# Storing the first chunk of results of a pooling kernel as soon as it is rooted

## The chip, the core and the metric

The kernel runs on one core of a Trainium2 chip. The metric is the device time of one execution in microseconds (us). Several executions are made and the median is quoted. A single core shows no pair of dies to compare, so a run's state ("fast" or "slow") is told only by its time against the fastest run of the same kernel: over 1.5% above it counts as slow.

Engines named below: ACT (ScalarE), DVE (VectorE), SP (SyncE, which here only issues DMAs). "ACTq" and "SPq" in the profile are the sequencers of ACT and SP issuing a DMA.

## The reference

```python
batch, channels, length = 32, 256, 4096          # x: float32, 134.2 MB
kernel_size, p = 4, 2.0
window = np.abs(x[:, :, start:end]) ** p          # four neighbours
result[:, :, i] = (np.mean(window, axis=-1)) ** (1.0 / p)   # out: 33.6 MB
```

The output is the root of the mean square of each four neighbours.

## The kernel before

The flat input is cut into 22 loads (18 of 13,184 columns on each of 128 partitions, four smaller ones at the end). The loads form 11 groups, mostly two loads each; a group's input and its output are contiguous in HBM for each partition. Each load is worked off in chunks: ACT squares in place, DVE sums four neighbours into the output tile, ACT takes the root. There are three input slots and two output tiles.

```python
W, O_W = 13184, 6592
X_SLOTS, O_SLOTS = 3, 2
slots = [[(W, [4416, 4384, 4384])]] * 18          # one load a slot, three chunks a load
...
groups = [2] * 9 + [3, 1]
late = {7, 8, 9, 10}                              # stored at the very end, from SP
...
def store(g, queue):
    queue.dma_start(out=block(of, g, k), in_=ots[g])

def root(g, o, ends):
    nc.scalar.activation(out=o, in_=o, func=Act.Sqrt, scale=1.0 / k)
    if ends and g not in late:
        store(g, nc.scalar)                       # one store a group, from ACT
...
for step in chunks:
    nc.scalar.activation(out=v, in_=v, func=Act.Square)
    nc.vector.tensor_reduce(out=o, in_=v.rearrange("p (n j) -> p n j", j=k), ...)
    if pending is not None:
        root(*pending)                            # the root of the chunk before
    pending = (g, o, ...)
```

Loads are issued from SP (`nc.sync.dma_start`), the stores of groups 0 to 6 from ACT. The two use different DMA queues (on the page q1 with 144.15 MB, the loads and the late stores from SP, and q10 with 23.63 MB, the stores from ACT).

## Time and profile before

| what | value | where it is read |
|---|---|---|
| time, median of 3 (394.69 to 394.88) | 394.79 us | runs |
| span of the profiled run | 393.0 us | page |
| bytes moved, mean rate | 167.79 MB, 427 GB/s | page |
| DVE busy, ACT busy | 72%, 74% | page |
| packets of one engine: 52,736 B (load), 26,368 B (store) | 1.947 us, 0.978 us | packet records of the trace |
| first packet starts, last one ends | 1.74 us, 391.71 us | packet records |

The first fence is the part of the page of the kernel before that cuts the span into 40 equal slices. The digits are tenths of busy time; DMA is the mean over sixteen DMA engines; the last row is what they moved.

```profile
DVE  0068989494959495949594959595859686899992
ACT  1099986777786768686958695959595949899991
DMA  8999999999999999999999999999999999999997
GB/s 344 429 429 440 429 424 381 443 459 429 413 440 435 429 427 432 429 440 441 437 448 421 432 462 435 392 429 472 429 413 451 425 429 429 424 429 427 438 429 329
```

The DMA row is 9 in all slices but the first and the last. DVE and ACT alternate between 9 and 4 to 6: they wait for data (ACT waited 86.3 us in sum for loads). So the kernel is bound by data movement. The packet records agree: 52,736 B in 1.947 us are 27.1 GB/s for an engine and 433 GB/s for sixteen, and 167.79 MB at that rate take 387.2 us of the 393.0.

The next fence is from the chain that ended last, in order of time: start, duration, what. (A line "issue" of 0.02 us before the last one is left out.)

```profile
123.51 4.73 DVE ot L110
128.26 39.98 DMA xt<-in_x_dram
168.26 3.88 ACT xt L108
```

It looks as if a load waited for DVE. It did: DVE freed an input slot and the load was issued at 128.26. But it took 40 us to land, while one load's bytes need 15.6 us at the full rate. Its first packet started at 148.56 us, 20.3 us after the issue: until then the packets of the load before it ran (128.13 to 147.45 us), and from 137.85 us on those of a store beside them. So, as an estimate from these times, a load could have been issued many microseconds later without landing later; compute has slack.

The DMA issues of the page: operands, sequencer, count, size of each, median us from issue to landing (all bytes have arrived).

```profile
xt<-in_x_dram SPq DMA_DIRECT2D x18, 6592.0 KB, 39.7
out_dram<-ot ACTq DMA_DIRECT2D x7, 3296.0 KB, 26.4
```

Last, two stretches early in the run and two around the first store (its packets run from 59.6 to 81.9 us): from:to, length, DVE busy, ACT busy, POOL busy, clock, DMA share, GB/s.

```profile
29.00:36.00 7.00, 6.45 (x2) 6.25 (x4) 0.00 (x0) 1.00 1.06 460
36.00:49.00 13.00, 11.87 (x4) 12.93 (x6) 0.00 (x0) 1.00 0.94 402
57.00:65.00 8.00, 7.40 (x3) 7.97 (x4) 0.00 (x0) 1.00 1.03 392
65.00:82.00 17.00, 11.50 (x3) 11.74 (x6) 0.00 (x0) 1.00 1.04 451
```

The engines are busy throughout, but at the beginning of the first store they move less. There the packet records show load packets of up to 3.1 us instead of 1.947; this is called the slow patch below. (Packets are counted where they start, so a short stretch can read above the full rate.)

### The profile page before, as it was taken

Reading aid. Unit: us, or ns where it says so; the run is one execution under the profiler, and the core shown is the slowest. Engines: PE = TensorE matmul, PEld = TensorE weight load, DVE = VectorE, ACT = ScalarE, POOL = GpSimd, SP = SyncE. Lnnn points to the kernel's source line nnn. Section 1 sums busy time; section 2 is a strip of 40 time slices with the busy share of each in tenths; the row PEclk is TensorE's granted clock in tenths of the full one; section 3 lists DMA queues with packets and bytes.
Section 4 is the critical chain, followed back from the end, with each engine's and each line's share of the span. In section 5 each row is a group of like instructions: output and inputs, shape, how many; then the busy total and the mean of one; then the engine's idle time right before and its main releaser. Section 6 shows DMA issues by size and latency. Waiting matters only on the chain.

```text
span 393.0 us, 316 instructions
## 1 busy us (share of the span) xinstructions
DVE 282.4 (72%) x62; ACT 292.4 (74%) x126; POOL 0.2 (0%) x4
## 2 busy tenths in 40 slices
DVE  0068989494959495949594959595859686899992
ACT  1099986777786768686958695959595949899991
POOL 0000000000000000000000000000000000000000
DMA  8999999999999999999999999999999999999997
GB/s 344 429 429 440 429 424 381 443 459 429 413 440 435 429 427 432 429 440 441 437 448 421 432 462 435 392 429 472 429 413 451 425 429 429 424 429 427 438 429 329
DMA packets 4754, 167.79 MB, mean 427 GB/s; under 512 B 528, under 2 KB 528, under 8 KB 656
## 3 DMA queue, kind: packets, MB, share of 16 engines
q1 hardware_dynamic: 3744, 144.15, 85.3%
q10 hardware_dynamic: 1008, 23.63, 14.0%
q14 instruction: 2, 0.02, 0.0%
HBM read 134.22 MB, written 33.55 MB: 427 GB/s over the span
## 4 chain that ended last, share of the span: by engine, by line
DMA 62%; ACT 19%; DVE 14%; issue 2%; ACTq 0%; SPq 0%
DMA xt<-in_x_dram 62%; ACT xt L108 15%; DVE ot L110 11%; DVE xt L110 3%; ACT ot L84 3%; ACT xt L84 1%; ACTq L81 0%; SPq L75 0%; ACTq L108 0%
## 5 line engine op out<-in xcount | busy, mean ns | idle before, releaser
L110 DVE TENSOR_REDUCE ot<-xt 128x1096 f32<-128x4384 f32 (+1 forms) x54 | 255.4, 4731 | 102.7 <-ACT xt L108 102.4
L108 ACT ACTIVATE xt<-xt 128x4384 f32<-128x4384 f32 (+3 forms) x62 | 230.3, 3716 | 89.2 <-DMA xt<-in_x_dram 86.3
L84 ACT ACTIVATE ot<-ot 128x1096 f32<-128x1096 f32 (+1 forms) x54 | 59.8, 1108 | 1.8 <-DVE ot L110 0.9
L110 DVE TENSOR_REDUCE xt<-xt 128x824 f32<-128x3296 f32 (+1 forms) x8 | 27.0, 3384 | 1.3 <-ACT xt L108 1.2
L84 ACT ACTIVATE xt<-xt 128x824 f32<-128x824 f32 (+1 forms) x8 | 6.7, 841 | 3.0 <-DVE xt L110 2.9
L108 ACT ACT_TABLE_LOAD x1 | 1.3, 1283 | 0.7 <-PEq L137 0.7
L84 ACT ACT_TABLE_LOAD x1 | 1.3, 1283 | 0.0
L137 POOL MEMSET const-bfloat16-1.0<- 128x1 bf16 x1 | 0.1, 101 | 0.0
L137 POOL MEMSET const-uint8-127<- 128x1 uint8 x1 | 0.1, 101 | 0.0
L137 POOL MEMSET const-float32-0.0<- 128x1 f32 x1 | 0.1, 98 | 0.2 <-issue 0.2
L137 POOL MEMSET const-float32-1.0<- 128x1 f32 x1 | 0.1, 98 | 0.0
## 6 DMA issues: line engine op xcount, KB each, us to landing
xt<-in_x_dram SPq DMA_DIRECT2D x18, 6592.0 KB, 39.7
out_dram<-ot ACTq DMA_DIRECT2D x7, 3296.0 KB, 26.4
xt<-in_x_dram SPq DMA_DIRECT2D x3, 3296.0 KB, 24.6
out_dram<-ot SPq DMA_DIRECT2D x2, 3296.0 KB, 29.6
xt<-in_x_dram SPq DMA_DIRECT2D x1, 2528.0 KB, 26.4
out_dram<-xt SPq DMA_DIRECT2D x1, 2472.0 KB, 9.3
out_dram<-xt SPq DMA_DIRECT2D x1, 632.0 KB, 5.0
```

The source lines that it names most:

```text
L84: nc.scalar.activation(out=o, in_=o, func=Act.Sqrt, scale=1.0 / k)
L108: nc.scalar.activation(out=v, in_=v, func=Act.Square)
L110: nc.vector.tensor_reduce(out=o, in_=v.rearrange("p (n j) -> p n j", j=k), axis=mybir.AxisListType.X, op=mybir.AluOpType.add,)
L137: nc = _bacc.Bacc("TRN2", target_bir_lowering=False, num_devices=1)
```

## The change

The results of the first chunk of group 0 (1,104 columns, 4,416 B per partition) are stored as soon as they are rooted, at about 30 us instead of 56 us. The rest of group 0 (21,952 B per partition) follows in a second store at the group's end. The intent is that stores begin earlier. All other groups are stored as before.

```diff
-    def store(g, queue):
-        queue.dma_start(out=block(of, g, k), in_=ots[g])
+    stored = {}
+
+    def store(g, queue, until=None):
+        first = stored.get(g, 0)
+        until = columns[g] // k if until is None else until
+        queue.dma_start(out=block(of, g, k)[:, first:until], in_=ots[g][:, first:until])
+        stored[g] = until
 
     def root(g, o, ends):
         nc.scalar.activation(out=o, in_=o, func=Act.Sqrt, scale=1.0 / k)
         if ends and g not in late:
             store(g, nc.scalar)
+        elif g == 0 and g not in stored:
+            store(g, nc.scalar, o.shape[1])
```

## The prediction

> **What bounds the kernel.** Data movement. On the page the DMA row reads 9 nearly everywhere; DVE is busy 72%, ACT 74% of the 393.0 us. Packet by packet, a load packet of 52,736 B takes 1.947 us and a store packet of 26,368 B 0.978 us in almost every case: 433 GB/s for sixteen engines. [...] 167.79 MB at 433 GB/s are 387.2 us. From the first packet (1.74 us) to the last end (391.7 us) the engines are idle for a fraction of a microsecond in sum. The other 5.8 us: 1.7 us before the first packet, 1.3 us after the last, about 2.0 us of packets slower than normal, and small per-packet costs. Slow packets sit in three places: the first load (0.65 us per engine), reads drifting slower at 36 to 56 us (0.26 us), and reads at 57 to 61 us, where the first store starts (0.99 us). No later store has such a patch.
>
> The chain of waits shows 62% DMA. Its ACT and DVE pieces are not exposed compute: each releases a load 40 us before that load lands, and the transfer queued ahead of it takes the first 20 us.
>
> **What the change does.** Bytes stay the same. The first store (26,368 B per partition, issued at 55.6 us) becomes 4,416 B at about 29.7 us and 21,952 B where it was: one DMA more.
> - DMA: 8 packets more per engine. From 26,368 B (0.978 us), 19,776 B (0.735 us) and 5,056 B (0.194 us) I estimate a fixed part of 7 ns in a packet, so 0.06 us in all.
> - ACT: one more issue, 0.37 us, and a drain of 0.1 us, at 30 us. About 10 us of slack there, so 0 on the path.
> - The added DMA rotates which completion semaphores later DMAs reuse; in the order of the instructions no load gets a wait on something recent.
> - The early 0.57 MB (1.3 us of the full rate) enters the read stream. [...] its eight 0.16 us packets per engine spread over about 17 us. Load 1 lands a few tenths later, load 2 about 1.3 us later, the rest of the store is 1.3 us shorter, so loads from the fifth on are where they were.
>
> **Critical path.** It is the sum of the packets. A store cannot fill idle DMA time, since there is none, and the last bytes are untouched. What can move is slow-packet time: the 0.99 us at the first store should move to 30 to 35 us, about unchanged, and the 0.26 us of drift may go, since after the first store none is seen. Sum: +0.06 - 0.25, about -0.2 us.
>
> **Predicted: 394.6 us, 8 in 10 between 393.7 and 395.6.** Faster by over 2%: 1%; within 2%: 98%; slower by over 2%: 1%.
>
> **What would show it.** Mean rate about 427 GB/s; DMA share 9 throughout; 128 data packets more on the ACT queue; 4,416 B packets of about 0.17 us starting near 31 us; one slow patch at 31 to 36 us and none at 57 us; last packets end at about 391.5 us; issues from the sixth load on within 0.5 us of before.
>
> **What would make it wrong.** If each of the two stores pays its own slow patch, about +1 us. If the patch scales with the first store's packets, about -0.8 us. [...] If a semaphore reuse holds a load back for over 15 us, more.

Passages that did not come from the traces of this case are cut and marked. +0.06 - 0.25 comes to -0.19 us, and 394.6 us stands as forecast. The "about 17 us" is the estimate from packet times, 8 x (1.947 + 0.16) us, as if each store packet of an engine waited for one load packet. The trace of the kernel before shows about that: while the packets of its second store ran (98.94 to 119.25 us), 112 load packets and 128 store packets started.

## The result and the profile after

The changed kernel took 394.92 us (median of 6, 394.78 to 395.09), the kernel before 394.80 us (median of 6, 394.69 to 395.12). The ratio is 1.0002, 95% interval 0.9989 to 1.0015: the same. (Here and below a ratio is the mean time of one kernel's fast runs over that of the other's of the same rounds, so not quite the ratio of the medians quoted.)

The slices of the changed kernel:

```profile
DMA  8999998999999999999999999999999999999997
GB/s 343 429 429 447 453 434 366 472 397 434 421 464 424 461 434 400 464 434 430 394 464 426 432 432 432 426 429 442 429 425 434 461 451 429 400 429 428 436 424 304
```

The DMA row is what it was but for one 8 at the seventh slice: there was no idle time for an early store to fill.

The beginning of the early store, from the timeline of the changed kernel (start, duration, engine, line, operation; in brackets the idle time before):

```profile
28.51 1.12 ACT L90 ACTIVATE ot<-ot 128x1104 f32<-128x1104 f32 x1
29.67 0.37 ACTq L86 DMA_DIRECT2D out_dram<-ot  x1
30.09 3.86 ACT L116 ACTIVATE xt<-xt 128x4384 f32<-128x4384 f32 x1 [0.45 <-ACT ot L90]
```

ACT loses 0.45 us, with no consequence. And the issues of the loads, of the stores of the other groups and of the two stores of group 0, in the columns used before:

```profile
xt<-in_x_dram SPq DMA_DIRECT2D x18, 6592.0 KB, 39.7
out_dram<-ot ACTq DMA_DIRECT2D x6, 3296.0 KB, 27.1
out_dram<-ot ACTq DMA_DIRECT2D x1, 2744.0 KB, 27.4
out_dram<-ot ACTq DMA_DIRECT2D x1, 552.0 KB, 20.7
```

This is the line to remember. The small store has a sixth of the bytes, and still needs 20.7 us to land against 27. Its packets start at 33.72 us and end at 48.14 us, 14.4 us for 0.57 MB that the engines could move in 1.3 us. In the stretch from 34 to 48 us the packet records hold 111 load packets (5.85 MB) and 108 store packets (0.48 MB): the two queues take turns packet by packet, although a load packet here has 52,736 B and a store packet 4,416 B.

The stretches that answer to those of before:

```profile
29.00:36.00 7.00, 5.89 (x2) 5.99 (x4) 0.00 (x0) 1.00 0.90 382
36.00:49.00 13.00, 12.17 (x3) 12.93 (x6) 0.00 (x0) 1.00 1.10 470
57.00:65.00 8.00, 7.47 (x2) 7.58 (x4) 0.00 (x0) 1.00 0.92 370
65.00:82.00 17.00, 12.05 (x4) 12.31 (x7) 0.00 (x0) 1.00 1.01 438
```

The dip is at 57 to 65 us still, where the second, large piece starts, although a store has already run at 34 to 48 us. The prediction had put it at 31 to 36 us. The low 382 GB/s at 29 to 36 us is not it: load packets slower than usual make only 0.1 us per engine there, and the two early stretches together move more than before (an effect of counting packets where they start).

What each part came to, in us per engine, worked out from the packet records (excess: packet times over the usual 1.947 us for load packets):

```
                                      before    after
store packets of group 0, 8 or 16       7.82     7.89    (0.978 | 0.171 + 0.815 each)
excess, first 20 us                     0.69     0.75
excess, 28 to 54 us                     0.26     0.22
excess, 56 to 66 us                     0.99     0.54
excess, whole run                       2.02     1.62
last packet ends at                   391.71   391.96
```

The slow packets became fewer by 0.4 us, the added packets cost 0.07 us, and yet the last packet ended 0.25 us later in the profiled run. Such sums are not good to a few tenths, because an engine's packets overlap at their edges (up to 19 were in flight on 16 engines), and the sixteen engines finish unevenly (within 0.6 us before, 1.0 us after). Time without a packet, between the first and the last, is 0.9 us per engine before and 1.5 us after, which is about what the sums leave open. The timed runs say that all of it together is nothing, to within 0.15%.

### The profile page after: what moved, and what is told of

Its sections match the earlier page's. It is cut to its first block, busy times and chain, and to the rows that moved or that the text cites. A ratio compares the mean times of both kernels' runs of the same rounds, so it can differ in the third digit from the quotient of the medians.

```text
span 393.3 us, 318 instructions
## 1 busy us (share of the span) xinstructions
DVE 282.4 (72%) x62; ACT 292.7 (74%) x126; POOL 0.2 (0%) x4
## 3 DMA queue, kind: packets, MB, share of 16 engines
q1 hardware_dynamic: 3744, 144.15, 85.1%
## 4 chain that ended last, share of the span: by engine, by line
DMA 58%; ACT 21%; DVE 16%; issue 2%; another core or an unknown queue 1%; ACTq 0%; SPq 0%
DMA xt<-in_x_dram 58%; ACT xt L116 17%; DVE ot L118 12%; DVE xt L118 3%; ACT ot L90 3%; ACT xt L90 1%; ACTq L86 0%; SPq L76 0%; ACTq L116 0%
```

## The experiments

Theory A: the DMA engines are never idle, the time is the sum of the packets, and when a store is issued does not matter. Rival B: an early start gains something, and the extra store loses as much. Later, theory R: the turns of the two queues decide when many small stores do harm; rival S: each added store costs a fixed time, by its issue, its semaphore or its small packets.

### The kernel before, again

No edit; a control for the noise and for the slow patch.

> The kernel before, unchanged, as a control: the size of the noise, and whether the slow patch of read packets at the first store (0.99 us per engine, at 57 to 61 us) comes back. Theory A (the DMA engines are never idle, so the time is the sum of the packets and the moment of a store does not matter): ratio 1.000 within 0.0015; total packet time per engine 390.3 us within 0.5. If the patch is of the schedule it is at 57 to 61 us again, 0.7 to 1.3 us; if it is chance it moves or changes by half.

It took 394.83 us, ratio 0.9998 (0.9986 to 1.0010). The slow patch came back at 56 to 61 us with 1.04 us per engine. So it belongs to the schedule and is not chance. The other excess is not so steady: the 0.26 us at 28 to 54 us is 0.01 us in this run of the same kernel.

### Two pieces, both at the group's end

```diff
         if ends and g not in late:
+            if g == 0:
+                store(g, nc.scalar, 1104)
             store(g, nc.scalar)
-        elif g == 0 and g not in stored:
-            store(g, nc.scalar, o.shape[1])
```

> The added store without the early start: group 0 is stored in the same two pieces, both at the group's end. Theory A: 394.9 us, equal to the changed kernel within 0.5 us. Rival B (an early start gains about 1 us, as much as the pieces of the early data, and the extra store [...] loses it again, so that the two cancel): here only the loss is left, about 396 us. The slow patch: if it belongs to the first store of any size, it is at 57 to 61 us before packets of 4,416 B; if it belongs to large store packets, it comes later, before those of 21,952 B.

It took 394.89 us, ratio 0.9998 (0.9986 to 1.0010). Rival B falls: without the early start there is no loss that a gain would have had to cancel. The slow patch now has 0.15 us at 58 to 66 us, among the packets of 4,416 B (57 to 72 us), and 0.68 us at 72 to 77 us, around the first of 21,952 B (from 74.5 us). In this run most of it comes with the first large store packets.

### The early piece dropped

```diff
         elif g == 0 and g not in stored:
-            store(g, nc.scalar, o.shape[1])
+            stored[g] = o.shape[1]
```

> The first chunk's results are never stored (a wrong result on purpose), the rest of group 0 as in the changed kernel. Theory A: the time falls by the packet time of the piece, 8 x 0.171 us = 1.4 us, to 393.5 us (ratio to before about 0.9967). Rival C (a rate limit that is not the sum of the packets, or a path elsewhere, on which the piece has no weight): no change, 394.9 us.

It took 393.61 us, ratio 0.9967 (0.9955 to 0.9979), 1.2 us less where 1.4 were expected. Rival C of the expectation falls: bytes count, and the piece's packet time is nearly what it is worth. This also bounds what any move of that piece could gain: not moving it at all gains 0.3%.

### Every chunk stored as it is rooted

The change carried through groups 0 to 6: 42 stores in place of 7.

```diff
-        elif g == 0 and g not in stored:
-            store(g, nc.scalar, o.shape[1])
+        elif g not in late:
+            store(g, nc.scalar, stored.get(g, 0) + o.shape[1])
```

> Every chunk of groups 0 to 6 is stored as soon as it is rooted: 35 stores more than before, 280 packets more per engine. Theory A, with 7 ns of fixed time in a packet: +2.0 us, 396.8 us (ratio 1.005), DVE and ACT waits larger but off the path. Rival B (early stores gain): under 394 us. If ACT's extra issues (about 0.45 us each, 16 us in sum) were on the path: over 400 us, which theory A excludes.

It took 429.36 us, ratio 1.0882 (1.0845 to 1.0920). Theory A missed by far: the loss was 34.6 us and not 2. Rival B missed too. "Over 400 us" was met in the number, but the 16 us of added issues that it rested on are not half of the loss. The slices of this run:

```profile
ACT  1299897125998834199999244999999900399994
DMA  9999999999999999978999998989999999139956
GB/s 381 401 459 435 424 424 424 424 429 399 416 376 449 424 425 439 412 308 330 363 440 463 452 430 375 352 372 413 424 433 420 426 429 426 81 121 412 412 235 295
```

The first 17 slices are full, then idle time appears, above all from 367 us on (slices 35, 36 and 39). In the packet records an engine is without a packet for 31 us in sum, against 0.9 us before. So "the DMA engines are never idle" is not a property of the kernel that stores leave alone. Its timeline around 84 to 105 us:

```profile
84.25 0.34 ACTq L86 DMA_DIRECT2D out_dram<-ot  x1
84.63 3.86 ACT L116 ACTIVATE xt<-xt 128x4384 f32<-128x4384 f32 x1 [10.27 <-DMA out_dram<-ot]
88.39 1.11 ACT L90 ACTIVATE ot<-ot 128x1104 f32<-128x1104 f32 x1
101.41 0.34 ACTq L86 DMA_DIRECT2D out_dram<-ot  x1
101.79 3.86 ACT L116 ACTIVATE xt<-xt 128x4384 f32<-128x4384 f32 x1 [12.29 <-DMA out_dram<-ot]
```

ACT stands at a store's issue until an older store has landed, and starts nothing else for 10 to 12 us; in the whole run it waited so seven times, 66.1 us in sum. (The DMAs of the program share eight completion semaphores in the traces. The store issued at 84.25 us has the semaphore of one that landed at 84.17, the store issued at 101.41 that of one that landed at 101.33.) The issues show why the older stores are late:

```profile
out_dram<-ot ACTq DMA_DIRECT2D x28, 548.0 KB, 38.2
out_dram<-ot ACTq DMA_DIRECT2D x14, 552.0 KB, 35.0
```

Stores of 0.56 MB take 35 to 38 us to land. Each of the first four stores has its packets spread over 14 us (33.5 to 47.6, 50.5 to 64.8, 67.5 to 81.9, 84.6 to 99.0), since each of an engine's 8 store packets waits for a load packet of 1.947 us. From 84 to 98 us the records hold 109 load packets (5.75 MB) and 126 store packets (0.56 MB). Three stores a load need 24 turns, and a load gives 8. The stores back up, ACT stalls, loads run out (from 103 to 111 us only stores move), and the compute that was held up is exposed at the end. This became theory R.

### Group 0 held back by one load

The opposite of the change, made from the kernel before.

```diff
+        rooted.append(g)
-        if ends and g not in late:
+        if ends and g not in late and g > 0:
             store(g, nc.scalar)
+        if len(rooted) == 9:
+            store(0, nc.scalar)
```

> The kernel before, with group 0's single store held back by one load (issued after the ninth chunk's root, about 75 us, instead of 55.6 us): the opposite of the change, and forty times the added ACT wait. Theory A (saturated DMA, slack in front of every load): 394.8 us within 0.5, though DVE must wait some 5 us for the output buffer that the late store holds. If the start of the stores were worth anything: the 3.4 MB that wait 20 us would cost more than 1 us. The slow patch of reads should move to about 76 to 81 us if it belongs to the first large store, and stay at 57 to 61 us if it belongs to the fourth load.

It took 394.89 us, ratio 1.0003 (0.9989 to 1.0017). The store was issued at 69.2 us, and DVE had to wait 12.4 us in one piece for the output tile (5 were expected); this did not reach the end either. So 3.4 MB stored 13.5 us later cost nothing measurable, as theory A has it. The slow patch moved with the store to 70 to 76 us, with 0.94 us: it does not belong to the fourth load.

### Two stores a group

```diff
-        elif g == 0 and g not in stored:
-            store(g, nc.scalar, o.shape[1])
+        elif g not in late and rooted[g] == 3:      # roots taken in this group
+            store(g, nc.scalar, widths[g])          # columns rooted in this group
```

> Two stores in each of groups 0 to 6, one after each load: packets of 13,184 B, 7 stores more than before. Theory R (of the run with every chunk stored, which lost 34.6 us where +2 was expected: the two queues take turns packet by packet, so while loads are queued a store gets one packet per load packet however small it is; three stores of 8 packets per load of 8 packets then fall behind, and the in-order ACT waits for old stores to land): one store per load just keeps up, each takes about 19 us to land, 395.2 us (+0.4 for the packets). Rival S (every added store costs about 1 us, 34.6 us over 35 stores, by issue, semaphore or packet): 7 us more, 401.8 us.

It took 394.91 us, ratio 1.0004 (0.9992 to 1.0017). Rival S, 7 us more, falls. Each store's packets span about 18 us, and a new store starts every 19.5 us: with one store packet per load packet the stores just keep up. (From issue to landing they take 25.6 us, where about 19 were expected.)

### Three stores a group

As the last one, with `rooted[g] in (2, 4)` in place of `== 3`.

> Three stores in each of groups 0 to 6, one after every second chunk: packets of 8.8 KB, 14 stores more than before. Theory R: 1.5 store packets per load packet are over what the turns allow, the backlog grows by half a store a load, from the third or fourth group on ACT waits for landings: over 400 us, 400 to 425. Rival S: +14 us, 409 us. A third view, that only the smallest packets are at fault: under 397 us. Together with the run of two stores per group it says whether there is an edge at one store packet per load packet.

Four runs took 398.73, 408.83, 409.24 and 410.51 us. The rule above calls the last three slow, but the clock is 1.0 in all four and the kernel before varied by 0.6 us in the same rounds, so this looks like two courses of this program itself. By the one fast run it is 1.0% slower than before; that misses "over 400", while the three others meet it. What sends a run the one way or the other was not found. None is under 397, so the view that only the smallest packets are at fault falls. The size of the loss at this number of stores is open; all four runs are above every run of the kernel before.

### Every chunk, in the loads' queue

The 42 stores again, issued from SP, so that they stand in line with the loads. (In the trace of the kernel before, all 26 DMAs issued from SP landed in the order of their issue.)

```diff
-            store(g, nc.scalar)
+            store(g, nc.sync)
         elif g not in late:
-            store(g, nc.scalar, stored.get(g, 0) + o.shape[1])
+            store(g, nc.sync, stored.get(g, 0) + o.shape[1])
```

> The same 42 small stores as in the run with every chunk stored, and as many DMAs, but issued from SP into the queue of the loads, first in first out, so that no turns are taken between two queues. Theory R: the backlog cannot form, and what is left is packet overhead: about +2.0 us, 396.8 us, at most 400. Rival S, or a theory in which the small packets or the reuse of completion semaphores alone are the cost: about 429 us again.

It took 404.08 us, ratio 1.0233 (1.0217 to 1.0249). The same small stores, as many DMAs, 25 us less than from ACT. This fits turns between the two queues as most of the loss, but the edit also takes the stores' waits off ACT; the pair below, which leaves all stores on ACT, tells the two apart. Its slices, against those of the twin above:

```profile
DMA  8999999989998999999999999999999999999986
```

But 397 was expected, and 7 us are left. The packet sum per engine is 7.2 us above that of before: 2.3 us in the store packets (336 of 0.170 us against 56 of 0.978), 0.5 us in store packets slower than that, and 4.4 us in load packets slower than usual. These are the last packets of a load, just before a run of small store packets. (Idle time rose from 0.9 to 3.4 us.) Theory R had no term for that; why those packets are slow was not tested.

### Two stores a load, whole and halved load packets

The stores do not differ within this pair. Both have four chunks a load and a store after every second one, 28 stores in all.

```diff
-    slots = [[(W, [4416, 4384, 4384])]] * 18
+    slots = [[(W, [3296, 3296, 3296, 3296])]] * 18
...
-        elif g not in late and rooted[g] == 3:
+        elif g not in late and rooted[g] in (2, 4, 6):
```

In the second of the pair each row of an input slot is two halves with a gap, meant to make two packets of 26,368 B of it (the lines that make the slot 32 columns wider and that read it in halves are left out):

```diff
...
+        if w == W:
+            v = slot_tiles[s].rearrange("p (h c) -> p h c", h=2)[:, :, 0:6592]
...
+        from_ = block(xf, g, 1)[:, src:src + w]
+        if w == W:
+            from_ = from_.rearrange("p (h c) -> p h c", h=2)
-        nc.sync.dma_start(out=v, in_=block(xf, g, 1)[:, src:src + w])
+        nc.sync.dma_start(out=v, in_=from_)
```

> Each load in four chunks instead of three; groups 0 to 6 stored in four pieces, one after every half load: packets of 6,592 B, 28 stores, two per load. Loads in packets of 52,736 B as before. Theory R (turns packet by packet, so that a store lasts as long as its 8 packets have to wait for load packets; over one store packet per load packet a backlog grows): well over the edge, 405 to 430 us, stores landing later and later, ACT, DVE or SP waiting for them. A rival for which one early store per half load is harmless: under 399 us.

> The same stores, chunks and number of DMAs as in the run with two stores per load, but each load's row in SBUF is two halves with a gap of 64 B, so that a load should be 16 packets of 26,368 B per engine instead of 8 of 52,736 B. Theory R: now there is one store packet per load packet, as in the run with two stores per group, so the stores keep up: 395 us plus about 2.2 us for 312 more packets per engine at 7 ns, 397 us, under 399. Rival S2 (the number of stores, the reuse of completion semaphores or the small store packets are the cause, whatever the load packets are): the same as its companion, over 403 us. If the trace shows load packets of 52,736 B still, the run says nothing.

With whole packets, four runs took 401.62, 411.48, 411.91 and 412.27 us (again two courses, at the same clock; the one that counts as fast is 1.7% above before, which misses the 405 to 430 expected, while the others meet it). With halved packets, 396.05 us (395.83 to 396.32), ratio 1.0031 (1.0018 to 1.0044). So the fast runs differ by 5.6 us, with a single one on one side. The trace shows load packets of 26,368 B, as intended (6,048 packets in the loads' queue instead of 3,744). First the issues with whole packets (this profile fell in one of the longer runs), then those with halved packets:

```profile
xt<-in_x_dram SPq DMA_DIRECT2D x18, 6592.0 KB, 24.9
out_dram<-ot ACTq DMA_DIRECT2D x28, 824.0 KB, 41.4
```

```profile
xt<-in_x_dram SPq DMA_DIRECT2D x18, 6592.0 KB, 39.3
out_dram<-ot ACTq DMA_DIRECT2D x28, 824.0 KB, 25.8
```

The stores are the same DMAs of the same size, and land in 25.8 us instead of 41.4. Their packets span 10 to 11 us each, where those of the first three stores of the other run span 17. Rival S2 falls, and theory R holds in both directions: with the same stores, the load packets' size decides whether they keep up. The 312 more packets per engine than before came with 1.24 us more time, 4 ns each, a little over half of the 7 ns that the prediction had estimated. (Their recorded times add up to 2.2 us more; packets overlap at their edges.)

### Two input slots: is an early store worth anything where the DMA engines are idle?

```diff
-    X_SLOTS, O_SLOTS = 3, 2
+    X_SLOTS, O_SLOTS = 2, 2
+    y_pool = ctx.enter_context(tc.tile_pool(name="y_pool", bufs=2))   # for the last two groups' results
```

> The kernel before with two input slots instead of three (the last two groups' results in a pool of their own), so that a load waits for the compute two loads back and the DMA engines stand idle at times: about 405 us (395 to 420), DMA share under 0.97 in the middle. It is the base of the pair with its changed twin.

> The changed kernel with two input slots. If an early store can fill idle DMA time, it can gain here at most the packet time of the piece, 1.4 us, against its twin: theory A expects 0 to 1.4 us faster than the twin, so a ratio between the two of 0.9965 to 1.000. A rival for which the early start is worth more than its bytes (a shorter tail, a smoother pipeline): over 2 us faster.

The twin of the kernel before took 434.36 us (ratio 1.0998, 1.0979 to 1.1018), that of the changed kernel 433.97 us (1.0980, 1.0958 to 1.1002). The estimate of 405 us for the base was far off: besides 27 us of idle time it has 15.9 us of load packets slower than usual per engine, most of them where loads start anew after an idle stretch or a large store starts. One of the six runs of the changed twin, 440.62 us, counts as slow and is left out. The pair is 0.2% apart (1.0980 over 1.0998), within both intervals; a gain of 0 to 1.4 us can neither be shown nor denied, and a gain of over 2 us is unlikely. The stretch where the early store finds idle engines, first the twin of before, then that of the changed kernel:

```profile
28.00:42.00 14.00, 12.53 (x4) 13.24 (x7) 0.00 (x0) 1.00 0.64 252
```

```profile
28.00:42.00 14.00, 10.88 (x4) 11.69 (x7) 0.00 (x0) 1.00 0.70 248
```

The engines are busier (0.64 to 0.70) and move no more per us, because the load under way slows down: its last packets, just before the first of the store at 34.4 us, take up to 3.4 us, and it ends at 36.2 instead of 34.7 us; the next starts at 39.6 instead of 39.0. That is a slow patch of 0.9 us per engine at a store of 4,416 B packets. The twin of before has none there.

No version that would beat both kernels came out of this. Before, 387.2 of the 393.0 us were bytes at the full rate, 3.0 us lay before the first and after the last packet, and at most 2 us were slow packets; a gain of 2% (7.9 us) is not there.

## Why the prediction was right, and where it was not

- **Bound by data movement, no idle time to fill: right.** The piece dropped altogether saved 1.2 us; held back or split without the early start, the store left the time unchanged.
- **Compute slack: right.** The added issue took 0.45 us of ACT, and even 12.4 us of DVE standing still did not reach the end.
- **Semaphores: right.** The DMAs of both kernels use eight completion semaphores, and the added store shifts which DMA has which (the load issued at about 109 us has number 100 before and 103 after). No load was held back by that in the changed kernel: SP's loads waited 24.6 us in sum for older loads, 26.1 us before. It is the run with every chunk stored where old stores hold up ACT (66.1 us).
- **Packet cost: right in the trace** (0.171 + 0.815 against 0.978 us, so 8 ns a packet, 0.07 us in all).
- **Turns of the two queues: right** (111 load packets beside 108 store packets from 34 to 48 us), with 14.4 us for the early store where 17 was estimated. Load 1 (the second) landed 0.4 us later, load 2 1.7 us later (1.3 was said). "Issues from the sixth load on within 0.5 us of before" did not quite hold: the sixth was issued 1.7 us later, the seventh 1.1 us, one more 0.6 us, and the others from the eighth on 0.4 us or less.
- **The failed step: "the 0.99 us at the first store should move to 30 to 35 us", and no patch at 57 us.** The patch stayed with the second, large piece (0.54 us at 58 to 66 us in the changed kernel, and 0.1 us at 28 to 37 us). The prediction took it for a cost of the first store of any kind. In the runs with three input slots and stores from ACT it came with the first store of 13 KB packets or more (at 72 to 77, 70 to 76 and 40 to 50 us), and three stores a group, of 8.8 KB packets, still had 0.8 us at 36 to 52 us. Packet size is not the whole condition, though: with two input slots the early store of 4,416 B packets had 0.9 us of it (31 to 34 us), and with all stores in the loads' queue the first small ones had 1.0 us (46 to 50 us). What these two share is that the slow packets are the last of a load, just before the store's. The shift was worth a few tenths and did not move the sum. What causes the patch is open.
- **The -0.2 us:** measured +0.12 us of the medians with an interval of about half a us either way. The sign was not settled. The -0.25 us in it rested on a drift seen in one profile: it stayed in the changed kernel (0.22 us at 28 to 54 us), and the control, the same kernel as before, has 0.01 us there, so it comes and goes from run to run. The time was met because all such terms are small beside the range, not because they were right.

The prediction missed a danger that the change is too small to meet: it stopped at "one DMA more" and did not ask what happens at three stores a load. The same turns that make the early store take 14.4 us went with a loss of 34.6 us there.

## What to carry to other kernels

Where the DMA row is full from end to end, as here, moving a store earlier or later gained nothing and cost nothing as long as the stores kept up (394.92 us with the early piece, 394.89 us with group 0 held back, 394.8 us before); only bytes, slow packets and the two ends of the run counted. Before cutting stores into small early pieces, count packets and not bytes. With loads and stores in two queues that took turns, a small store of 8 packets an engine took about as long as 7 or 8 load packets of 1.947 us (14.4 us for 0.57 MB). With one store a load the stores kept up (394.91 us). With three (24 store packets to 8 load packets an engine) they backed up until ACT stood 10 to 12 us at an issue for an old one (429.36 us). If early small stores are wanted, make the load packets as small in proportion (two stores a load took 396.05 us with halved load packets, 401.62 us at best with whole ones), or put fewer stores in.
